# A decoder step: every second store of the finished y of groups 0 and 1 on ScalarE's queue, with new instruction orders

## The chip, the cores and the metric

The kernel runs on one core of one Trainium2 chip. The metric is device time in microseconds (us) of one execution. Before the change three runs gave 1998.69, 1999.23 and 3230.68 us; their median, 1999.23, is the time before. Engines are named as in the profile: PE is TensorE's matrix multiplication, PEld its weight load, DVE is VectorE, ACT is ScalarE, POOL is GpSimd, SP is SyncE, which here only issues DMAs.

## The reference, cut to what matters

One step of a decoder layer, in fp32, over 2048 prompt tokens and 8 sample tokens (2056 in all), with D_MODEL 1024 and D_FF 2816:

```python
def _rmsnorm(x, g):
    return x * lax.rsqrt(jnp.mean(x * x, axis=-1, keepdims=True) + EPS) * g

def _layer(x, ...):
    z = _rmsnorm(x, norm1_g) @ w_in          # split: RG-LRU branch, gelu gate, q, k, v
    rec = rglru(causal_conv(xr)) * gelu(gr)  # gated linear recurrence over the tokens
    att = sliding_window_attention(q, k, v)  # itself and 128 tokens back, learned sinks
    mix = concat(_rmsnorm(rec, rec_norm_g), _rmsnorm(att, attn_norm_g))
    h = x + mix @ w_out
    hn = _rmsnorm(h, norm2_g)
    y = h + (silu(hn @ w_gate) * (hn @ w_up)) @ w_down
    return y, ...

y_prompt = _rmsnorm(yp, final_norm_g)        # the same for y_sample
```

The change touches the last two lines, the feed-forward network (FFN) with its residual and the final norm. The caches and states that the step also returns are left out here.

## The kernel before

**Layout.** Activations are held transposed: 128 partitions are 128 features, the free dimension is tokens. An fp32 matrix product is done as three PE products of a high and a low part (hi x hi, hi x lo, lo x hi), so each weight tile is made as a pair: ACT casts the high part (L1903 in `keep_weights`, L1972 in `split_parts`), and POOL or DVE subtracts it to get the low part (L1904, L1973).

**Phases.** Up to some 600 us the kernel works on the input projection, the two head groups and the output projection; their result h goes to DRAM (`hs`). The rest is the FFN over three groups of tokens (`HALVES`): group 0 has 688 tokens, groups 1 and 2 have 684, each in two halves of 344 or 342 (n = 0, 1). Within a group, eleven pairs (`NPAIR`) of 128-wide chunks of D_FF are worked off:

- `mixed_weights` loads the weights of a pair; in group 0 it makes sums of their blocks and stores them to DRAM (`split_g`, `split_u`), from where groups 1 and 2 load them (L1927, 512 KB each).
- `products` multiplies gate ("g") and up ("u") by a Strassen-like scheme with seven block products instead of eight, in the order of `PRODS` = 1, 2, 6, 5, 7, 3, 4. Each is 12 matmuls into a PSUM bank. ACT copies the banks of products 1, 6 and 5 out (L2110, L2115, L2117), DVE adds the others.
- `down_parts` multiplies the result by w_down in the same way, in 14 rounds, each with two outputs of three matmuls. After each one DVE adds the PSUM bank into the tile y (L2175). Four of these chains share a set of PSUM banks, so a round can begin only when DVE has emptied the bank that it writes to. Pair 10 of each group and the first three pairs of group 0 use the plain `down` with 16 products (L2146).

**y.** The 16 pieces of y of a group (8 chunks of 128 features by 2 halves, 128 x 344 fp32 or 172 KB each) lie three to a tile in six tiles of the pool `bigp`. `y_load` (L1893 to L1899) loads them from h in DRAM, the residual; the down products are added to them; `finish` (L2177 to L2196) norms and stores them. `finish` runs once for each half of groups 0 and 1 and is called f01, f00, f11 and f10 (group, half; half 1 is done first, since the last `down` makes it first). For each half it squares and adds up the eight pieces, has PE sum over the partitions, and brings the row of norms over all partitions with `dram_bcast`: the row goes to DRAM and comes back broadcast as `rb_f` (L1152 to L1157). Then for each of the eight pieces DVE multiplies by gain and norm (L2195, a scalar_tensor_tensor), and SP stores the piece to the output (L2196). The tile is then used for the next group's y, whose load has to wait until the stores of the old pieces in it have landed. So at the passage from group 0 to 1 and from group 1 to 2, 16 multiplications, 16 stores and 16 loads meet the first products of the next group. Group 2 has a function of its own, `finish_last`, which already issues every second store of half 0 on ACT (L2243).

**The order of the work.** Each engine works off its instructions in order, and that order is written out by hand: `ORDER` (L106 to L852) is a dictionary with a list for each of PE, DVE, ACT, POOL and SP; `order` and `order_engines` (L1079 to L1095) turn the lists into dependencies. The tokens are these:

- On DVE, ACT, POOL and SP a token is the name of a chain, the generator that makes the instruction: `f11` is `finish` of group 1, half 1; `y2` is `y_load` of group 2; `wu2.1` is `mixed_weights` of up, group 2, pair 1; `wd2.0` the down weights, `pu2.1` `products` of up, `d2.0` `down_parts` of group 2, pair 0. Each token takes the next instruction that this chain has on this engine; `+k` takes the one that stands k further on among those left, and `:n` takes n in a row.
- On PE a token is a product: `u2_1_4:10` is ten matmuls of up, group 2, pair 1, product 4; `g2_2_1` is gate of pair 2; `w2_0_6_1:3` the three matmuls of the down round of product 6, column 1, group 2, pair 0; `st_` and `tr_` are the small ones of the norms.

The same lists also give the number of filler matmuls (`FILLS`, L854) that PE runs in the first 100 us while weights are being split.

A store that goes to another queue is thus in another engine's list: it must be named in ACT's list and vanish from SP's. An instruction that issues a DMA waits on its engine until the data is there, and all that stands behind it in that engine's list waits too.

Of the kernel before, what the change touches and what calls it, by code (L numbers as in the profile page):

```python
# [961 lines left out]
def hybrid_step(tc, xT, xR, vecs, cst, gatew, win, wout, wgate, wup, wdown, kT, vC, ck, cv, sconv, sh0,  # L962
                yT, pkT, pvT, pconv, phs, skw, svw, sconv_o, sh_o):
    nc = tc.nc
# [3 lines left out]
    with ExitStack() as ctx:  # L968
# [888 lines left out]
        with ExitStack() as bctx:  # L1857
# [319 lines left out]
            def finish(gi, n, t, dt):  # L2177
# [14 lines left out]
                for m in range(KD):  # L2192
                    yield t + dt * (F_FIN[2] + F_FIN[3])
                    v = ys[gi, n, m]
                    nc.vector.scalar_tensor_tensor(v, v, col(V_GF + m), bc[:, :nn], ALU.mult, ALU.mult)  # L2195
                    nc.sync.dma_start(yT[:, m, o:o + nn], v)  # L2196
# [187 lines left out]
```

## Time and profile before

| what | value |
|---|---|
| runs | 1998.69, 1999.23, 3230.68 us; median 1999.23 |
| profiled execution | 1999.11 us, of which the span of the profile is 1997.0 us |
| mean granted clock of PE | 0.997 of full speed |
| PE busy | 1971.0 us, 99% of the span, 12112 matmuls |
| DVE busy | 1560.6 us, 78% |
| ACT, POOL busy | 981.3 us, 49%; 959.8 us, 48% |
| DMA | 461.93 MB, 231 GB/s on average over the span |
| L2196, the stores | 32 instructions, issued by SP from 1137.5 to 1602.5 us |

The run of 3230.68 stands alone; the profiled execution agrees with the other two. PE is the engine to look at: where it idles, the end of the kernel moves, and where another engine idles, that tells nothing by itself. In rows by stretch, the first column is the stretch in us from the start of the span, then its length, then the busy time of PE, weight load, DVE, ACT and POOL with the count of instructions, then the granted clock, the share of the DMA engines and GB/s. In a timeline row the first figure is the start of a run of like instructions in us, the second their length, then engine, line, operation, output and inputs, form and count; the brackets give the idle time ahead of it and what ended it. "SPq" and "ACTq" are the parts of SP and ACT that issue DMAs. In rows of waits stand the waiting instruction, what released it, and then total us, count and longest.

### The profile page before, as it was taken

The numbers are of one execution on the slowest core, as the hardware profiler recorded it, in microseconds if no ns is written. First come the engines' busy times: TensorE is split into PE (matmuls) and PEld (weight loads), VectorE is DVE, ScalarE is ACT, GpSimd is POOL, SyncE is SP. The second block draws the span as 40 slices with busy tenths as digits, with TensorE's granted clock in tenths as the row PEclk, the third lists the DMA queues.
The fourth block names the chain that finished last, engine by engine and source line by source line (L and its number), as shares of the span: only waits on it lengthen the run. The fifth ranks groups of instructions, "written<-read, shape, count | busy, mean of one in ns | idle before, by whom it ended". The sixth has DMA issues, their size and how long they took to land. (4 is left out here: it accounts for less than half of the span.)

```text
span 1997.0 us, 34846 instructions
## 1 busy us (share of the span) xinstructions
PE 1971.0 (99%) x12112; PEld 1874.8 (94%) x12112; DVE 1560.6 (78%) x2894; ACT 981.3 (49%) x2032; POOL 959.8 (48%) x821
## 2 busy tenths in 40 slices
PE   8999999999999999999999999999999999999998
PEld 8988898888877999999999999999999999999998
DVE  7887986777986888888998786886668586766776
ACT  6775774664664534444446433433345433433433
POOL 5412362130233896788998754534456423322323
PEclk9999999999999999999999999999999999999999
DMA  8873586576688978655667886776558675565552
GB/s 314 287 252 138 194 300 198 183 254 210 223 283 291 335 263 268 220 215 210 246 241 279 265 289 231 234 237 210 191 191 267 228 259 199 179 211 195 180 181 103
DMA packets 218470, 461.93 MB, mean 231 GB/s; under 512 B 26230, under 2 KB 90406, under 8 KB 218278
## 3 DMA queue, kind: packets, MB, share of 16 engines
q1 hardware_dynamic: 214662, 456.69, 67.4%
q10 hardware_dynamic: 3632, 3.02, 0.4%
q8 instruction: 95, 1.56, 0.3%
q14 instruction: 81, 0.66, 0.1%
HBM read 345.51 MB, written 115.17 MB: 231 GB/s over the span
## 5 line engine op out<-in xcount | busy, mean ns | idle before, releaser
L1070 PE MATMUL ps_g<-hn,w_g 128*128 128x342 f32 (+1 forms) x2772 | 569.4, 320 | 0.3 <-DMA w_g<-split_g 0.3
L1070 PE MATMUL ps_u<-hn,w_u 128*128 128x342 f32 (+1 forms) x2772 | 559.5, 320 | 1.5 <-DMA w_u<-split_u 0.9
L1070 PEld LDWEIGHTS ps_g<-hn,w_g 128*128 128x128 f32 x2772 | 461.3, 188 | 1.2 <-ACT wd L1972 0.5
L1070 PEld LDWEIGHTS ps_u<-hn,w_u 128*128 128x128 f32 x2772 | 459.5, 188 | 3.0 <-ACT c_u L2115 1.6
L2175 DVE TENSOR_TENSOR y<-y,pw 128x342 f32<-128x342 f32 (+1 forms) x756 | 359.1, 504 | 114.7 <-PE pw L1070 108.4
L1070 PE MATMUL ip<-xn,w_in 128*128 128x512 f32 (+1 forms) x1680 | 365.2, 357 | 6.1 <-ACT xn L1105 5.7
L1070 PEld LDWEIGHTS ip<-xn,w_in 128*128 128x128 f32 x1680 | 269.6, 189 | 45.8 <-ACT xn L1105 5.7
L1070 PE MATMUL pw<-fh,wd 128*128 128x342 f32 (+1 forms) x864 | 253.4, 320 | 0.5 <-DVE y L2175 0.5
L1070 PE MATMUL pw<-t,wd 128*128 128x342 f32 (+1 forms) x972 | 243.7, 320 | 2.8 <-DVE y L2175 2.7
L1070 PE MATMUL op<-mix,w_out 128*128 128x512 f32 (+1 forms) x960 | 205.8, 355 | 0.4 <-ACT mix L1544 0.4
L1070 PEld LDWEIGHTS op<-mix,w_out 128*128 128x128 f32 x960 | 157.5, 189 | 25.3 <-ACT mix L1544 0.8
L1070 PEld LDWEIGHTS pw<-t,wd 128*128 128x128 f32 x972 | 169.9, 188 | 4.9 <-DVE y L2175 4.0
L1973 POOL TENSOR_TENSOR wd<-rd,wd 128x512 fp32r<-128x512 f32 x85 | 121.8, 1434 | 103.4 <-ACT wd L1972 99.1
L1972 ACT CAST wd<-rd 128x512 fp32r<-128x512 f32 x159 | 98.6, 621 | 130.0 <-PE ps_u L1070 39.8
L1070 PEld LDWEIGHTS pw<-fh,wd 128*128 128x128 f32 x864 | 158.6, 188 | 1.2 <-DVE y L2175 0.8
L1904 POOL TENSOR_TENSOR w_u<-ru,w_u 128x512 fp32r<-128x512 f32 x44 | 61.4, 1395 | 170.2 <-ACT w_u L1903 95.9
L1070 PE MATMUL pw<-fl,wd 128*128 128x342 f32 (+1 forms) x432 | 132.9, 320 | 0.0
L2089 DVE TENSOR_TENSOR c_u<-c_u,ps_u 128x342 f32<-128x342 f32 (+1 forms) x99 | 50.2, 508 | 101.2 <-PE ps_u L1070 93.9
L2071 POOL TENSOR_TENSOR c_u<-c_u,c_g 128x342 f32<-128x342 f32 (+1 forms) x60 | 65.4, 1090 | 124.8 <-DVE c_u L2089 115.1
L2060 DVE TENSOR_TENSOR fl<-c_u,fh 128x342 fp32r<-128x342 f32 (+1 forms) x132 | 105.4, 803 | 17.7 <-ACT fh L2059 17.0
L2059 ACT CAST fh<-c_u 128x342 fp32r<-128x342 f32 (+1 forms) x132 | 63.0, 480 | 110.6 <-POOL c_u L2071 49.3
L1070 PE MATMUL pd<-fh,w_d 128*128 128x344 f32 (+1 forms) x384 | 92.9, 320 | 0.0
(319 smaller groups left out, 3490.7 us busy)
## 6 DMA issues: line engine op xcount, KB each, us to landing
w_g<-split_g SPq DMA_DIRECT2D x88, 512.0 KB
w_u<-split_u SPq DMA_DIRECT2D x88, 512.0 KB
w_in<-split_w SPq DMA_DIRECT2D x84, 512.0 KB
rg<-in_wgate SPq DMA_DIRECT2D x110, 256.0 KB
ru<-in_wup SPq DMA_DIRECT2D x110, 256.0 KB
w_out<-split_w SPq DMA_DIRECT2D x48, 512.0 KB
split_g<-w_g SPq DMA_DIRECT2D x44, 512.0 KB
split_u<-w_u SPq DMA_DIRECT2D x44, 512.0 KB
```

The costliest lines, as they stand in the source:

```text
L1070: r = nc.tensor.matmul(*args, **kw)
L1904: lo_eng.tensor_tensor(w[:, 1, :], src, w[:, 0, :].bitcast(F32), op=ALU.subtract)
L1972: nc.scalar.copy(w[:, :, 0], v)
L1973: eng((E_DLO0, E_DLO1, E_DLO2)[gi][j]).tensor_tensor(w[:, :, 1], v, w[:, :, 0].bitcast(F32), op=ALU.subtract)
L2059: nc.scalar.copy(hi, v)
L2060: nc.vector.tensor_tensor(lo, v, hi.bitcast(F32), ALU.subtract)
L2071: (nc.vector if p == NPAIR - 1 or src is not v else eng(E_MUL[2 * h + n])).tensor_tensor(v, src, g, op=ALU.mult)
L2089: nc.vector.tensor_tensor(o, a, b, op)
L2175: nc.vector.tensor_tensor(v, v, ps, ALU.add)
```

## The change

One line of code changes, in `finish`: the pieces with odd m are stored by ACT's queue, the even ones still by SP's. That is 4 stores of each of f01, f00, f11 and f10, 16 in all. All five lists of `ORDER` are replaced: SP's has 1471 entries instead of 1487, ACT's 1903 instead of 1887, the others have the same instructions in another sequence. Most of the text of the lists differs only in where lines break; instructions really change places at the start (up to 50 us), around 550 to 650 us, in pairs 6 to 8 of group 0, and at the two passages between groups. The diff, cut to the code line and the lists at these passages:

```diff
@@ finish @@
                     nc.vector.scalar_tensor_tensor(v, v, col(V_GF + m), bc[:, :nn], ALU.mult, ALU.mult)
-                    nc.sync.dma_start(yT[:, m, o:o + nn], v)
+                    (nc.scalar if m % 2 else nc.sync).dma_start(yT[:, m, o:o + nn], v)
@@ ORDER, PE, group 1 to 2 @@
-u2_1_2:11 tr_f1_0 u2_1_2 u2_1_6:12 w2_0_2_0:3 u2_1_7:11 u2_1_5:12 u2_1_7 u2_1_3:12 u2_1_4:7 g2_2_1 u2_1_4 g2_2_1
-u2_1_4:4 w2_0_6_1:3 w2_0_6_0:3 g2_2_1:7 w2_0_1_3:2 g2_2_2 w2_0_1_3 g2_2_1:2 g2_2_2 g2_2_1 g2_2_2:9 w2_0_7_0:3 g2_2_2
-w2_0_7_1:3 w2_0_6_3:3 w2_0_3_0:3 w2_0_4_0:3 w2_0_3_1:3 w2_0_2_1:2 w2_0_4_1:3 w2_0_2_1 w2_0_5_2:3 w2_0_1_2:3 w2_0_7_3:3
+u2_1_2:11 tr_f1_0 u2_1_2 u2_1_6:12 w2_0_2_0:3 u2_1_7:11 u2_1_5:12 u2_1_7 u2_1_3:12 w2_0_6_1:3 w2_0_6_0:3 w2_0_1_3:3
+w2_0_7_0:3 w2_0_7_1:3 w2_0_6_3:3 w2_0_3_0:3 w2_0_4_0:3 w2_0_3_1:3 w2_0_2_1:2 w2_0_4_1:3 w2_0_2_1 w2_0_1_2:2 w2_0_7_3:2
+w2_0_1_2 w2_0_7_3 u2_1_4:2 w2_0_5_2:3 w2_0_2_2:3 u2_1_4:10 g2_2_1:2 g2_2_2 g2_2_1 g2_2_2 g2_2_1:2 g2_2_2:2 g2_2_1
...
@@ ORDER, DVE, group 0 to 1 @@
-f00+6 f00+5 f00+4 wu1.1 f00+3 f01 pu1.1 f00 d1.0 f00 wd1.0 d1.0+9 f00 pu1.0 d1.0+3 d1.0 wd1.0 f01 d1.0+2 d1.0+10
-d1.0:2 d1.0+2 d1.0 d1.0+9 d1.0+1 wd1.0 pu1.1+1 d1.0+1 d1.0+1 d1.0 d1.0+1 d1.0+8 pu1.1 d1.0+3 pu1.1+4 wg1.2 d1.0:2
+f01 f01+1 wu1.1 f00+5 f00+2 f00+5 f00+4 pu1.1 pu1.0 d1.0 f00+1 f00 wd1.0+1 f00 d1.0+9 d1.0 wd1.0+1 wd1.0 d1.0+2 f00
+pu1.1+1 d1.0+2 d1.0+10 f01 d1.0 d1.0+12 d1.0+3 d1.0 d1.0+2 d1.0 wd1.0 d1.0+1 d1.0:2 d1.0+1 d1.0+8 d1.0 d1.0+2 pu1.1
...
@@ ORDER, DVE, group 1 to 2 @@
-pg2.1 f10 pu2.0+1 wu2.1 wd2.0 pu2.0 pg2.1 pu2.0 pg2.1 wd2.0 f11+7 f11+2 f11+2 f11+3 pu2.1 f11+3 f11+2 f11:2 pu2.1+1
-f10+2 f10+4 f10+5 f10+4 f10 f10+2 d2.0+1 f10 d2.0 wg2.2 f10 d2.0+8 pu2.1+2 wg2.2 pu2.1+2 wd2.0 pu2.1+3 d2.0+2 d2.0+2
+pu2.0:2 pu2.0+1 f11 wu2.1 pu2.0+2 pu2.0:2 pg2.1 f10 pu2.0+1 wu2.1 wd2.0 pu2.0 pg2.1 pu2.0 pg2.1 wd2.0 f11+7 f11+3
+f11+3 f11+2 f11:2 f11+1 f11 pu2.1 f10+5 f10+2 f10+5 f10+4 f10+2 f10+1 d2.0 f10 d2.0 f10 pu2.1+1 pu2.1+2 pu2.1+2 d2.0+8
...
@@ ORDER, ACT, group 0 to 1 @@
-pg1.1 pu1.0 f00 wd1.0 wu1.1 pg1.1+2 pu1.1 wd1.0+1 wd1.0 pu1.0 wd1.0+1 pu1.1+1 wd1.0 pg1.1 pu1.1+1 wu1.1 pg1.1 wg1.2
+pg1.1 wd1.0+1 pg1.1 pu1.0+1 pu1.0 f00 wd1.0 wu1.1 f01+3 f01+2 pg1.1+2 pu1.1 wd1.0:2 f01 f00+2 pu1.0 f00+2 pu1.1+1
+pu1.1+1 f00 wd1.0 f00 f01 wd1.0 pg1.1 wu1.1 wg1.2 pu1.1 wg1.2 wd1.1 pu1.1 pg1.1 pg1.2 wd1.1:2 pu1.1:4 pg1.2+1 wd1.1
...
@@ ORDER, ACT, group 1 to 2 @@
-wu2.1 pu2.0 wd2.0 pu2.0+1 pu2.0 pg2.1+1 wu2.1 pg2.1:2 wd2.0 pu2.0 f11 pg2.1 wd2.0 pg2.1 wd2.0 pu2.1 pg2.1 f10 pu2.1+1
-wd2.0+1 pu2.1+1 wu2.1 wg2.2 wd2.0 wg2.2 pg2.2 wd2.1+1 pu2.1 wd2.1 pu2.1:2 wd2.1 pg2.2+1 pu2.1:2 wg2.2 pu2.1 wd2.1
+pg2.1:2 wd2.0 pu2.0 f11 pg2.1 wd2.0 pg2.1 wd2.0 pu2.1 f11+3 f10 f11 pu2.1+1 pg2.1 f11+1 pu2.1+1 f10+2 f10+2 f10+1 f10
+f11 wd2.0+1 wd2.0 wu2.1 wg2.2:2 wd2.1+1 pg2.2 pu2.1 wd2.1 pu2.1:2 wd2.1 pg2.2+1 pu2.1:2 wg2.2 pu2.1 wd2.1 pg2.2+1
...
@@ ORDER, SP, group 0 to 1 @@
-wd1.0+2 wd1.0+1 wd1.0+1 mix2 wg1.1 wu1.1 mix2 wg1.1 wd1.0+1 mix2:2 mix2+3 wg1.2 wu1.1+4 mix2+5 f01:2 wu1.1 f00 wd1.0+2
-mix2+3 wu1.1 f01+4 f00 f01+6 f01+1 wd1.1 f01+4 f01+1 wd1.0+1 wu1.1 f00+2 y1 f00+6 f00+5 f00+4 f01+2 y1:3 y1+1 y1+1
-y1+3 y1+4 y1+1 y1+1 f00+1 y1+1 f00 wd1.1+2 wg1.2 f01 y1 f00:2 f01 wu1.1 y1+1 wd1.1+1 wd1.1 y1 y1+1 y1 wg1.2 wg1.2+3
+mix2 wg1.1 wu1.1 mix2 wg1.1 wd1.0+2 mix2+5 mix2+1 mix2 wd1.0+1 wg1.2 wu1.1+4 mix2+5 f01 mix2+3 f01 wu1.1 f00 wd1.0+2
+wu1.1 wd1.1 f00 f01+3 f01+1 wd1.0+1 wu1.1 y1 f01+1 f00+1 y1+1 f00+2 y1:2 y1+2 y1+2 y1+3 y1+4 f01 wu1.1 y1+2 f00:2
...
@@ ORDER, SP, group 1 to 2 @@
-wd2.0:2 wg2.1:4 wd2.0 wg2.2 wd2.0:2 wu2.1+4 wd2.1 f11 wu2.1 f11 wg2.2 wd2.1 wu2.1+1 wu2.1 f11+7 f10 f11+2 wu2.1 f11+4
-f10 f11+2 f11+3 y2+2 f11+2 y2 f11+1 f11 y2 f10+2 f10+4 f10+5 f10+4 f10 f10+2 f10 y2 y2+2 y2+4 y2+5 y2+3 f10 y2+2 y2+2
+wu2.1+4 wd2.1 f11 wu2.1 f11 wg2.2 wd2.1 wu2.1+1 wu2.1 f10 wu2.1 f10 f11+2 y2+1 y2:2 f11+2 f11+1 f10+1 f10+2 y2 y2+2
+y2+4 y2+5 y2+2 f11 y2+2 f10+1 f10 y2+2 y2 wg2.2 y2+1 y2+3 y2+1 y2 wd2.1:3 wg2.2+1 wg2.2+2 y2 wd2.1 wg2.2 wd2.1 wu2.2
...
```

In words, at group 1 to 2: PE runs the twelve matmuls of up product 4 of pair 1 and the start of the next gate behind most of the down rounds of pair 0 (`w2_0_...`) instead of ahead of them; on ACT the eight stores stand among the casts and PSUM copies; on SP the stores that stood between the loads of up weights (`wu2.1`) are fewer. At group 0 to 1, PE's list moves four matmuls of up product 3 (pair 1) ahead of the last down rounds of pair 0; DVE's and SP's lists mix stores, loads of y and adds in another sequence.

More of the change, by code (lines that the diff above doesn't have):

```diff
@@ new lines @@
+pu0.9+3 pu0.9+1 d0.8 d0.9+1 pu0.9 pg0.10 d0.9 wd0.9 d0.9:2 wd0.9+1 pu0.9+1 pu0.9+1 wd0.9 pu0.9:2 d0.9 pg0.10 d0.9
+wu0.10 pg0.10 d0.9 d0.9+3 pu0.9 d0.9+1 d0.9:2 d0.9+4 d0.9+1 d0.9+1 d0.9+1 d0.9+2 wu0.10 d0.9+3 d0.9+2 d0.9+1 wd0.9
+wu0.10:2 d0.9 d0.9+2 d0.9+2 d0.9:2 pu0.10:2 hn1 wg1.0 d0.9 pu0.10 d0.9 d0.9+1 d0.9 hn1 pu0.10:2 pu0.10+1 hn1 pu0.10+1
+pu0.10:2 hl1 pu0.10:2 pg1.0 d0.10:3 hl1 d0.10:2 f01 d0.10:2 d0.10+1 d0.10 hl1 d0.10 hl1 d0.10 f01 f00 d0.10 d0.10+2
+wu1.0 f00 pg1.0 d0.10+1 d0.10 f01 d0.10 pg1.0 f01 f00 pu1.0 f00 mix2+1 mix2 wg1.1 mix2 pu1.0 mix2 pu1.0 pu1.0+1
@@ new lines @@
+pu0.9 wd0.9:2 wg0.10 pu0.9 wg0.10+1 pu0.9+2 wg0.10 wd0.9 pu0.9 pg0.10+1 pg0.10:2 pu0.9 wd0.9 wu0.10 pu0.9 wd0.9
+pg0.10:2 wu0.10 wu0.10+2 pg0.10 wd0.9 wu0.10:4 pu0.10 hn1:2 wg1.0 pu0.10 hn1+1 hn1 pu0.10 hn1+1 wg1.0 hn1+1 pu0.10
+wd0.10 hl1 wd0.10 hn1 hn1+1 hn1 wd0.10 hn1:2 pg1.0 pu0.10 hn1 pu0.10 hl1+2 hl1 wd0.10 pu0.10 hl1 hl1+2 hl1+1 hl1
+pg1.0+1 f01 hl1+1 hl1 f01+1 f01 wg1.0 hl1+2 pg1.0 hl1 f01 hl1:3 f00 hl1+1 wu1.0 hl1 f00 wu1.0 f00 f01:2 f00 pg1.0 f01
+f00 f01 f00 pg1.0:3 f00 wu1.0 f00 pu1.0 wg1.1:2 pu1.0+1 pu1.0:2 pg1.1 pu1.0 wg1.1 wd1.0 pu1.0 wu1.1 pu1.0 pg1.1+1 f01
@@ L771 @@
[L771 to L774 removed]
+pu0.9 wg0.10 wd0.9:3 wu0.10:3 wu0.10+1 wu0.10 wd0.9 wu0.10+1 wu0.10 hn1 wg1.0 hn1:2 hn1+1 hl1 wd0.10 hn1:5 wd0.10:3
@@ L775 @@
+hl1+3 hl1+1 hl1+1 hl1+1 f01 hl1 wg1.0 hl1+2 hl1+1 wu1.0 hl1 f01 f00 hl1 hl1+1 hl1 wd1.0 f01 f00 wd1.0+4 f00 wu1.0
+wg1.1 pu1.0:3 wd1.0 wg1.1 wu1.1 f01 pu1.0:2 f00 wd1.0:2 wd1.0+1 pu1.0 wd1.0+1 wd1.0+1 wd1.0 wd1.0+1 wd1.0 pu1.1 wu1.1
+pu1.1 wg1.2 wd1.1+5 wd1.1 wd1.1+1 wd1.1:2 pu1.1:3 wd1.1:2 pu1.1 wd1.1:2 wg1.2 wd1.1+1 wu1.2 wd1.1 wd1.2 wd1.2+4
+wd1.2+1 wd1.2+1 wu1.2 wg1.3 pu1.2 wd1.2 wd1.2+2 wd1.2+2 pu1.2 wd1.2 wd1.2+2 pu1.2 wd1.2 pu1.2:3 wg1.3 wd1.2 wu1.3:2
 wg1.4 pu1.3 wd1.3 pu1.3 wd1.3:2 pu1.3:4 wg1.4 wu1.4 wd1.3 wu1.4 wg1.5 pu1.4 wd1.4:2 pu1.4:4 wd1.4 pu1.4 wg1.5 wd1.4
@@ L852 @@
+wd2.7 wg2.9 wu2.8+4 wd2.8 wg2.9 wd2.8 wu2.8 wd2.8 wd2.8+1 wu2.8 wd2.8 wu2.8:2 wg2.9+4 wu2.9 wd2.8 wg2.9:2 wd2.8 wg2.9
+wu2.9 wg2.9 wd2.8 wg2.10 wu2.9+4 wg2.10 wd2.9:3 wu2.9 wd2.9:2 wu2.9:3 wg2.10+4 wu2.10 wd2.9+1 wg2.10:2 wd2.9 wg2.10
+wu2.10 wg2.10 wd2.9 wd2.10 wu2.10+4 wd2.10:2 wu2.10:3 wd2.10 wu2.10 f21:5 f21+1 f21+1 f21 f20:4
 """,
```

1350 lines of the change are left out of this document (666 added, 684 removed).

## The prediction

> **What bounds the kernel now.** I read the page's engine table first, then the busy time by stretches of the span, then the waits of TensorE (PE) in each stretch that has idle time, and last the timelines of the two places that the change touches.
>
> ```profile
> PE 1971.0 (99%) x12112; PEld 1874.8 (94%) x12112; DVE 1560.6 (78%) x2894; ACT 981.3 (49%) x2032; POOL 959.8 (48%) x821
> 10.00:100.00 90.00, 88.03 (x708) 85.61 (x707) 73.00 (x152) 65.30 (x141) 45.45 (x43) 1.00 0.88 305
> 1140.00:1160.00 20.00, 17.18 (x99) 15.14 (x98) 18.21 (x36) 5.30 (x11) 6.15 (x7) 1.00 0.94 302
> 1160.00:1580.00 420.00, 420.00 (x2679) 419.72 (x2678) 305.14 (x544) 174.06 (x361) 212.21 (x182) 1.00 0.68 227
> 1580.00:1615.00 35.00, 32.76 (x202) 31.03 (x201) 26.13 (x50) 8.94 (x19) 8.78 (x7) 1.00 0.91 292
> 1615.00:1950.00 335.00, 335.00 (x2134) 334.96 (x2134) 240.37 (x452) 130.26 (x258) 101.68 (x85) 1.00 0.59 195
> ```
>
> In the rows by stretch the first figures are the stretch and its length, then the busy time of PE, weight load, DVE, ACT and POOL, the granted clock, the DMA share and GB/s. PE is busy 1971.0 of 1997.0 us, so 26.0 us are all that any edit outside PE can win. The stores of groups 0 and 1 fall into 1140 to 1160 and 1580 to 1615, where PE idles 20.00 - 17.18 = 2.8 us and 35.00 - 32.76 = 2.2 us. Between and after them it idles 0.0 us. The change can therefore win at most 5.0 us there, 0.25%, while every us of new wait is paid in full, since PE has no slack to make it good. One matmul costs 335.00/2134 = 0.157 us.
>
> ```profile
> PE pw L1070 <- DVE y L2175: 1.9, 3, 0.7
> PE ps_u L1070 <- DMA w_u<-split_u: 0.9, 1, 0.9
> PE pw L1070 <- DVE y L2175: 1.4, 2, 1.2
> PE ps_u L1070 <- ACT c_u L2117: 0.4, 1, 0.4
> PE ps_g L1070 <- DMA w_g<-split_g: 0.3, 1, 0.3
> ```
>
> These are PE's waits, total, count, longest: two lines of the first stretch and three of the second. Most of it, 3.3 us, is PE waiting for DVE to add a down product into y (L2175) and so to free its PSUM bank. DVE is late because the 16 final multiplications (L2195) and the loads of the next y stand in its way.
>
> **What the change does to the queues.** 16 of the 32 stores of L2196 go from SP's queue to ACT's.
>
> ```profile
> L2196 SPq DMA_DIRECT2D out_yT<-y x32: 332/388/705, 1137.5 to 1602.5; - x32
> L2243 ACTq DMA_DIRECT2D out_yT<-y x4: 339/374/749, 1991.2 to 1992.8; - x4
> ```
>
> Shortest, median and longest issue in ns: SP sheds 16 x 0.388 = 6.2 us of issuing, ACT takes on 16 x 0.374 = 6.0 us, 3.0 us at each place. ACT is busy 5.30 of 20 us and 8.94 of 35 us there, so this lies beside PE and costs 0. What can cost is the order: ACT runs in order, and behind a store that waits for DVE's multiplication stand copies of PSUM that PE itself waits for (the 0.4 us above).
>
> The first place, SP's side:
>
> ```profile
> 1142.14 0.40 SPq L1927 DMA_DIRECT2D w_u<-split_u  x1
> 1144.52 2.21 SPq L2196 DMA_DIRECT2D out_yT<-y  x4
> 1147.09 6.03 SPq L1899 DMA_DIRECT2D y<-hs  x9
> SPq L1899 <- DMA w_u<-split_u: 0.9, 1, 0.9
> 1155.00:1160.00 5.00, 4.94 (x28) 4.41 (x29) 4.90 (x12) 1.01 (x2) 0.71 (x1) 1.00 1.02 330
> ```
>
> The nine y loads take 6.03 us to issue, 0.67 each instead of 0.39, and one of them waits 0.9 us for a weight load with which it shares no data: SP may have only so many transfers in flight, and the DMA engines are full (share 1.02 at 330 GB/s). A store is 172 KB, so 176/330 = 0.53 us of DMA time whichever queue issues it.
>
> [...]
>
> **The sum, first transition (group 0 to 1).** Before the w_u load at 1142.14 SP's old list has five stores of f01 behind the load of the product before it, the new list two. That brings the load forward by between 0 and 3 x 0.53 = 1.6 us, and its wait of 0.9 falls to between 0.9 and 0; I take 0.2. But this gain does not reach the end. Behind it PE waits three times for DVE's adds:
>
> ```profile
> 1149.47 0.50 DVE L2175 TENSOR_TENSOR y<-y,pw 128x342 f32<-128x342 f32 x1
> 1154.49 3.63 DVE L2175 TENSOR_TENSOR y<-y,pw 128x342 f32<-128x342 f32 x8
> 1155.05 1.21 PE L1070 MATMUL pw<-t,wd 128*128 128x342 f32 x6 [0.73 <-DVE y L2175]
> ```
>
> PE's third wait ends at 1155.05 with the add at 1154.49, which stands ten places behind the add at 1149.47. In the new DVE list the first add has two multiplications fewer ahead of it and one other operation more, 1.0 - 0.5 = 0.5 us earlier at best; but between the two adds stand eleven operations instead of nine, two at about 0.5 us. So the fifth add, and with it PE, comes out between 0.5 us early and 1.0 us late. I take 0.3 late. PE's list also moves four matmuls of up product 3 ahead of the last w rounds, which needs its weights some 4 us sooner; SP's list moves the load from behind 24 y loads and stores to behind 12 of them, 12 x 0.53 = 6.4 us sooner at best. I take 0 with a bound of +0.5. First transition: +0.3, from -0.9 (the w_u wait gone and nothing in its place) to +1.5.
>
> **Second transition (group 1 to 2).** Here the orders change more.
>
> ```profile
> 1593.65 3.26 PE L1070 MATMUL ps_u<-hn,w_u 128*128 128x342 f32 x19 [0.44 <-ACT c_u L2117]
> 1599.26 0.74 PE L1070 MATMUL pw<-t,wd 128*128 128x342 f32 x3 [1.24 <-DVE y L2175]
> 1600.16 0.73 PE L1070 MATMUL pw<-t,wd 128*128 128x342 f32 x3 [0.16 <-DVE y L2175]
> 1590.04 0.32 SPq L1156 DMA_DIRECT2D rb_f<-rows_f  x1
> 1583.15 2.03 DVE L2195 SCALAR_TENSOR_TENSOR y<-y,vec,rb_f 128x342 f32<-128x342 f32 x4 [0.77 <-DMA rb_f<-rows_f]
> 1594.07 4.71 DVE L2195 SCALAR_TENSOR_TENSOR y<-y,vec,rb_f 128x342 f32<-128x342 f32 x6
> 1598.70 0.50 DVE L2175 TENSOR_TENSOR y<-y,pw 128x342 f32<-128x342 f32 x1
> 1594.20 1.60 POOL L1904 TENSOR_TENSOR w_u<-ru,w_u 128x512 fp32r<-128x512 f32 x1 [3.12 <-DVE c_u L2089]
> ```
>
> Now PE runs up product 3 (12 matmuls from 1593.65), then product 4 and two matmuls of the next gate, 14 x 0.157 = 2.2 us, and only then w2_0_6_1, where it waits 1.24 us for the add at 1598.70. The new list puts all 14 behind the w rounds, because ACT's cast of product 4's weights now stands behind five stores. So PE arrives at w2_0_6_1 at 1593.65 + 12 x 0.157 = 1595.5.
>
> When is DVE there? Its six multiplications begin when the row broadcast has landed, 1594.07 now, 4.0 us after its issue. SP's list loses the three stores that stood between w_u loads ahead of that broadcast: 0 to 3 x 0.53 = 1.6 us sooner, I take 0.9, so 1593.2. Four multiplications take 2.03 us, 0.49 each; the six at 1594.07 took 4.71 while POOL ran beside them (1594.20). POOL's operation there subtracts the high part of a weight that ACT casts, and ACT's list has that cast later now, so I take 6 x 0.49 = 2.9, with 4.7 as the bound. Then come one add, a multiplication and the add that PE waits for: 0.42 + 0.49 + 0.50 = 1.4. That is 1593.2 + 2.9 + 1.4 = 1597.5, between 1596.8 and 1600.2: PE waits 2.0 us (1.3 to 4.7). After six matmuls (0.9 us) it needs the next bank, whose add stands behind a multiplication and three adds or products on DVE, 0.49 + 4 x 0.42 = 2.2 us: another 1.2 us (0.5 to 1.5). Against 1.24 + 0.16 + 0.28 = 1.7 now, the last being the wait for w_g, whose matmuls move back: +1.5, from +0.1 to +4.5.
>
> **The rest.** The new lists also permute single instructions in the first 100 us, around 550 to 650 and in pairs 6 to 8 of group 0. At the start SP loads the second half of a weight (256 KB, 0.8 us at 330 GB/s) ahead of an x tile, and some filler matmuls move. PE idles 2.0 us in 10 to 100. I take 0, bounded by one such transfer either way and rounded up: -1.0 to +1.0.
>
> **Sum.** The profiled execution took 1999.11 us, its span 1997.0 and 2.1 around it; the median of the runs is 1999.23, 0.1 above. 1999.1 + 0.3 + 1.5 + 0 = **2000.9 us**, no difference that a measurement of this kernel tells from none (about 2%, 40 us).
>
> **The rivals.**
>
> *The stalls go.* The y loads of the next group start sooner because half the stores no longer stand in front of them, and DVE's adds find their y and their turn. For it: 3.3 us of PE's waits are for these adds, and the new SP lists have y loads directly behind the second or third store. Against it: in 1155 to 1160 DVE is busy 4.90 of 5.00 us, so its adds wait for DVE's turn rather than for data. All waits gone would be 1999.1 - 2.8 - 1.7 = 1994.6; half of them gone, which I take, 1996.9.
>
> *Only issue time is saved.* The transfers are what is full, the stores' new queue changes nothing, and PE's and DVE's new orders cost and win alike. Then half of the 0.9 us wait for w_u goes: 1998.7. [...]
>
> *The clock drops: slower.* One long wait of PE costs more than itself:
>
> ```profile
> PE bc_at L1070 <- ACT rb_at L1140: 2.4, 1, 2.4
> 220.00:225.00 5.00, 5.00 (x18) 4.16 (x19) 3.74 (x7) 3.49 (x7) 1.75 (x3) 0.66 0.03 14
> ```
>
> After the single wait of 2.4 us before it, the stretch 220 to 225 was granted 0.66 of the clock: 0.34 x 5 = 1.7 us more. [...] The point from which it decides is a wait at w2_0_6_1 of 2.4 us or more, that is DVE's add after 1597.9, only 0.4 later than I take it. ACT can bring that about as well: if a store at its head holds up the PSUM copy ahead of product 3. With a wait of 3.5, midway between 2.4 and 4.7: 3.5 + 1.2 - 1.7 + 1.7 + 0.3 = +5.0, so 2004.1. For it: the bounds reach far above it; against it: the three waits of 0.5 to 0.7 us at 1150 to 1155 came in pieces and left the clock at 1.00.
>
> **How the numbers follow.** Forecast 0.40, with its own range 1999.2 to 2003; stalls go 0.18; issue time alone 0.20; clock drop 0.22. The range takes in the first two rivals' times and most of the third's bounds: 1996.6 to 2005.2, which leaves out under 0.2, the fuller win towards 1994.6 and waits near the upper bounds with the clock drop. All four lie within 2%. For over 2% either way 40 us would have to come from somewhere: a win of 40 exceeds all idle time, 26.0, so 0.005; a loss of 40 would need a hold-up that repeats in every pair, where the orders are nearly unchanged, so 0.015; within 2% 0.98.
>
> **What would show it.** Right: out_yT issues on ACT, 16 of them, about 0.4 us each; in the second transition one PE wait of about 2 us for DVE y directly behind up product 3 and a second near 1.2, with w_g's 0.3 gone; in the first the wait for w_u under 0.5 and the sum of PE idle near 3 us; 0.0 idle between and after. Wrong: PE idle under 1.5 us in both stretches together with y loads landing sooner (first rival), a clock row under 1.00 behind 1600 (third), PE waiting for an ACT copy for over 1 us, or idle time that appears where nothing of the stores is near.

## The result and the profile after

The changed kernel took 2003.39 us (median of 17 runs) against 1999.08 of before (17 runs beside them). The ratio is 1.0024, interval 1.0017 to 1.0031: 4.8 us slower, from 3.4 to 6.2. The single runs of 3230.68 us here and of 2749.80 in one of the experiments stand far from all others and are left out of the ratios. The result lies within 2% and inside the range given, but it is not the forecast of +1.8: it is near that of the third rival, the clock drop, at +5.0. The profiled execution took 2005.35 us, its span 2003.5.

The rows by stretch of the changed kernel, cut as for before (stretch, length, busy PE, weight load, DVE, ACT, POOL, clock, DMA share, GB/s), under the page's engine row:

```profile
PE 1974.9 (99%) x12112; PEld 1880.3 (94%) x12112; DVE 1556.0 (78%) x2894; ACT 980.2 (49%) x2032; POOL 956.1 (48%) x821
...
1140.00:1160.00 20.00, 16.85 (x92) 15.45 (x92) 17.84 (x33) 4.17 (x9) 6.71 (x6) 0.91 0.93 305
1160.00:1580.00 420.00, 420.00 (x2678) 419.63 (x2678) 303.58 (x547) 174.38 (x363) 211.91 (x182) 1.00 0.69 227
1580.00:1615.00 35.00, 29.95 (x170) 28.39 (x169) 22.48 (x44) 7.41 (x16) 7.42 (x6) 0.90 0.83 275
1615.00:1950.00 335.00, 335.00 (x2134) 334.96 (x2133) 239.82 (x452) 130.91 (x260) 101.66 (x85) 1.00 0.59 196
```

As before, PE idles nowhere between and after the two passages. Inside them two things are new. PE idle grows from 2.2 to 5.05 us in the second passage and by 0.3 in the first. And the granted clock, 1.00 in both places before, is 0.91 over the first 20 us and 0.90 over the second 35. PE's *busy* time grew by 3.9 us with the same 12112 matmuls: matmuls that run slower count as busy, so the busy share does not show this loss; the clock column does. In short stretches of the second passage:

```profile
1600.00:1602.50 2.50, 1.65 (x6) 1.21 (x6) 2.47 (x6) 1.78 (x4) 1.08 (x1) 0.72 0.76 237
1602.50:1605.00 2.50, 1.46 (x5) 1.46 (x6) 2.03 (x5) 0.41 (x1) 2.50 (x3) 0.50 0.93 267
```

In steps of 0.25 us the clock falls to 0.50 at 1601.1 and is back at 1.00 at 1607.9.

The stores moved as the diff says, 16 to each queue:

```profile
L2196 ACTq DMA_DIRECT2D out_yT<-y x16: 338/339/397, 1138.9 to 1600.3; - x16
L2196 SPq DMA_DIRECT2D out_yT<-y x16: 332/386/544, 1139.8 to 1604.2; - x16
```

PE's waits, first passage and then second:

```profile
PE ps_u L1070 <- ACT c_u L2115: 1.2, 1, 1.2
PE pw L1070 <- DVE wd L1973: 1.0, 1, 1.0
PE pw L1070 <- DVE y L2175: 0.9, 2, 0.7
...
PE pw L1070 <- DVE y L2175: 4.5, 2, 3.2
PE ps_u L1070 <- ACT c_u L2117: 0.4, 1, 0.4
```

The timeline of the second passage, by engines (start, length, work, count; in brackets the idle time ahead):

```profile
1595.26 2.14 PE L1070 MATMUL ps_u<-hn,w_u 128*128 128x342 f32 x12 [0.44 <-ACT c_u L2117]
1600.58 1.65 PE L1070 MATMUL pw<-t,wd 128*128 128x342 f32 x6 [3.18 <-DVE y L2175]
1603.55 0.65 PE L1070 MATMUL pw<-fh,wd 128*128 128x342 f32 x1 [1.31 <-DVE y L2175]
1604.56 2.77 PE L1070 MATMUL pw<-t,wd 128*128 128x342 f32 x9
1612.23 1.72 PE L1070 MATMUL ps_u<-hn,w_u 128*128 128x342 f32 x10
...
1596.19 3.00 DVE L2195 SCALAR_TENSOR_TENSOR y<-y,vec,rb_f 128x342 f32<-128x342 f32 x6 [7.26 <-DMA rb_f<-rows_f]
1600.02 0.50 DVE L2175 TENSOR_TENSOR y<-y,pw 128x342 f32<-128x342 f32 x1
...
1596.80 3.88 ACTq L2196 DMA_DIRECT2D out_yT<-y  x5
1601.77 0.61 ACT L1903 CAST w_u<-ru 128x512 fp32r<-128x512 f32 x1
...
1603.80 1.28 POOL L1904 TENSOR_TENSOR w_u<-ru,w_u 128x512 fp32r<-128x512 f32 x1
```

And two rows of the kernel before that were not shown:

```profile
1593.50 0.62 ACT L1903 CAST w_u<-ru 128x512 fp32r<-128x512 f32 x1
...
1601.96 0.32 PE L1070 MATMUL pw<-fh,wd 128*128 128x342 f32 x1
```

The passage begins 1.60 us later than before (ACT's first PSUM copy in it starts at 1585.00 instead of 1583.40). With that taken off, PE's two rounds behind DVE's adds start at 1598.98 and 1601.95. In the kernel before these were 1599.26 and 1601.96: **nearly the same two moments.** The first is set by DVE's add in both kernels. The second is set by DVE only now; before, PE came to it behind seven matmuls without a wait. In a second trace of the changed kernel, shown further down, the two rounds start 1.3 and 1.7 us earlier than before, counted from the start of the passage, and the passage is slow all the same. So it is not the rounds that come late. What differs is what PE does until then. Before, it ran 14 matmuls ahead of the first round and seven between the two; now it runs none: its new list has them behind the rounds, and up product 4's weights are cast behind five stores (1601.77 instead of 1593.50). The 21 matmuls, 21 x 0.157 = 3.3 us, come later and cover nothing. Then the nine matmuls at 1604.56 take 2.77 us, at a granted clock of 0.50; in "fill, both" below, at 1.00, the same nine take 1.59.

### The profile page after: what moved, and what is told of

The parts are those of the page before. It is cut to its first block, busy times and chain, and to the rows that moved or that the text cites. A ratio compares the mean times of both kernels' runs of the same rounds, so it can differ in the third digit from the quotient of the medians.

```text
span 2003.5 us, 34849 instructions
## 1 busy us (share of the span) xinstructions
PE 1974.9 (99%) x12112; PEld 1880.3 (94%) x12112; DVE 1556.0 (78%) x2894; ACT 980.2 (49%) x2032; POOL 956.1 (48%) x821
## 4 chain that ended last, share of the span: by engine, by line
PE 93%; DVE 4%; DMA 2%; ACT 1%; issue 1%; POOL 0%; SPq 0%; DVEq 0%; ACTq 0%; POOLq 0%
PE ps_g L1070 21%; PE ps_u L1070 21%; PE pw L1070 18%; PE ip L1070 14%; PE op L1070 7%; PE pd L1070 5%; PE s L1070 1%; PE o L1070 1%; PE pt L1075 1%; PE g L1070 1%; DMA split_g<-w_g 1%; DVE xc L1457 1%; DVE y L2195 0%; DMA n<-hs 0%; DMA mixed<-n 0%
## 5 line engine op out<-in xcount | busy, mean ns | idle before, releaser
L1973 POOL TENSOR_TENSOR wd<-rd,wd 128x512 fp32r<-128x512 f32 x85 | 121.2, 1426 | 110.9 <-ACT wd L1972 110.9
L1903 ACT CAST w_g<-rg 128x512 fp32r<-128x512 f32 x99 | 60.9, 621 | 67.4 <-PE pw L1070 24.0
```

What stands on the lines that cost most here:

```text
L1903: nc.scalar.copy(w[:, 0, :], src)
L1973: eng((E_DLO0, E_DLO1, E_DLO2)[gi][j]).tensor_tensor(w[:, :, 1], v, w[:, :, 0].bitcast(F32), op=ALU.subtract)
```

## The experiments

Theory A: the new orders of PE and DVE, most of all in the second passage, uncover waits for DVE, and the clock drops behind them. Theory B: ACT's queue costs. Rival C: the waits alone cost, the clock is a sign of them. Rival D: late transfers and casts cost.

Whole executions scatter by some 2 us, as much as what is looked for, so each trace is also read between marks. (A trace shows one execution, and in several kernels one of the shorter ones: 2001.19 us against a median of 2004.32 in "changed, again", 1999.45 against 2001.11 in "fill, both".) The first passage is counted from ACT's copy L2110 of gate pair 1 to that of up pair 2 in group 1, the second from up pair 1 to gate pair 3 in group 2. Line numbers of some experiments are one higher or lower. In before the marks are

```profile
L2110 ACT COPY c_g<-ps_g x1: 445/445/445, 1119.3 to 1119.3; 128x342 f32<-128x342 f32 x1
...
L2110 ACT COPY c_u<-ps_u x1: 447/447/447, 1193.9 to 1193.9; 128x342 f32<-128x342 f32 x1
...
L2110 ACT COPY c_u<-ps_u x1: 446/446/446, 1583.4 to 1583.4; 128x342 f32<-128x342 f32 x1
...
L2110 ACT COPY c_g<-ps_g x1: 445/445/445, 1649.9 to 1649.9; 128x342 f32<-128x342 f32 x1
```

so 74.6 and 66.5 us. For all kernels (ratio to before with interval; "new" where the passage has all or some of the changed orders):

| kernel | ratio | first passage | second passage |
|---|---|---|---|
| before | 1 | 74.6 | 66.5 |
| changed | 1.0024 [1.0017, 1.0031] | new 75.7 | new 71.4 |
| changed, again | 1.0018 [1.0009, 1.0026] | new 76.2 | new 70.4 |
| first passage only | 1.0005 [0.9996, 1.0014] | new 75.6 | 67.4 |
| second passage only | 1.0019 [1.0011, 1.0028] | 74.4 | new 70.9 |
| queue only | 1.0006 [0.9997, 1.0015] | 74.8 | 67.5 |
| orders only | 1.0038 [1.0024, 1.0052] | new 76.9 | new 72.6 |
| PE and DVE, second | 1.0032 [1.0021, 1.0044] | 74.2 | new 73.9 |
| fill, second | 1.0020 [1.0011, 1.0028] | new 76.2 | filled 69.9 |
| fill, both | 1.0012 [1.0002, 1.0022] | new 76.3 | filled 68.7 |
| first, stores late | 1.0022 [1.0012, 1.0032] | new 76.0 | 66.3 |
| first, load behind | 1.0007 [0.9998, 1.0016] | new 76.2 | 66.0 |
| PE and DVE, first | 1.0051 [1.0038, 1.0064] | new 85.2 | 67.1 |
| fill far away | 0.9997 [0.9988, 1.0006] | 74.8 | 66.8 |

**Which passage, queue or order.** Four kernels take the change apart: one passage or the other, the queue without the orders, the orders without the queue. In the passage kernels and in "queue only" the store's line is

```diff
-                    nc.sync.dma_start(yT[:, m, o:o + nn], v)
+                    (nc.scalar if m % 2 and gi in (0,) else nc.sync).dma_start(yT[:, m, o:o + nn], v)
```

with (0,), (1,) or (0, 1); "orders only" leaves that line as before and takes the changed lists.

> The kernel before with only the group 0 to 1 passage of the changed one: the stores of f01 and f00 with odd m on ACT's queue and all five orders of that passage. Everything else as before. In the profiled execution of the changed kernel this passage costs 1.25 us against before: 0.33 us more PE idle and a granted clock of 0.91 in 1140 to 1160. Theory A (the new orders cost, mostly in the group 1 to 2 passage): +1.2 us, ratio about 1.0006, clock below 1.00 somewhere in 1150 to 1160. Theory B (ACT's queue itself costs, the same at both passages): +2 us, half of the whole +4.3.

> The kernel before with only the group 1 to 2 passage of the changed one: the odd stores of f11 and f10 on ACT's queue and all five orders of that passage (and the few permutations behind it). Theory A: this passage carries the loss, +4.9 us or ratio 1.0025: one PE wait of about 3.2 us for DVE's add behind up product 3, a second of 1.3, and a clock near 0.5 for some 6 us after it. Theory B: +2 us, half of the whole.

> The orders of before on PE, DVE and POOL, and on SP and ACT too except that the 16 odd stores are taken out of SP's list and put into ACT's at the place where SP issued them in the profile of before. Theory A: nothing, -0.5 to +0.5 us, since PE's 14 matmuls stay ahead of the wait for DVE's add. Theory B: about +4 us as in the changed kernel, because ACT's copies and casts stand behind stores. If it is faster by 1 us or more, the queue does what the first rival of the prediction said (the y loads come sooner).

> All five orders of the changed kernel, but the 16 odd stores stay on SP's queue: they are taken out of ACT's list and put into SP's at the place where ACT issued them in the profile of the changed kernel. Theory A: as slow as the changed kernel, +4 us or ratio about 1.002, with the same long PE wait at the group 1 to 2 passage and the same clock drop. Theory B: 0.

Measured: +1.0 us (-0.8 to +2.8) for the first passage alone, +3.8 (2.2 to 5.6) for the second, +1.2 (-0.6 to +3.0) for the queue alone, with both passages at the upper end of what the old orders took elsewhere (74.2 to 74.8, 66.0 to 67.4), and +7.6 (4.8 to 10.4) for the orders alone. That is theory A. Theory B falls as the main cause: with the stores on SP the new orders do at least as badly. What the queue costs by itself cannot be told from nothing. The stretches of the two passages, first in "orders only" and then in "queue only":

```profile
1140.00:1160.00 20.00, 16.97 (x83) 15.28 (x83) 17.58 (x34) 3.04 (x6) 4.69 (x4) 0.83 0.93 293
1595.00:1610.00 15.00, 10.77 (x43) 10.14 (x44) 12.35 (x27) 1.57 (x3) 2.42 (x2) 0.66 0.78 250
```

```profile
1140.00:1160.00 20.00, 17.11 (x101) 15.44 (x100) 19.25 (x35) 4.64 (x10) 6.73 (x6) 1.00 0.96 323
1595.00:1610.00 15.00, 13.14 (x70) 12.39 (x70) 13.09 (x24) 3.74 (x7) 4.06 (x3) 0.89 0.93 308
```

The last column but two is the clock: under the new orders it falls in both places, under the old ones with the stores on ACT only a little, in the second (in before it stands at 1.00 in both).

**PE's and DVE's orders by themselves, second passage.** The lists of PE and DVE are the changed ones from the passage on, all else is before:

```diff
 PE
-u2_1_3:12 u2_1_4:7 g2_2_1 u2_1_4 g2_2_1 u2_1_4:4 w2_0_6_1:3 w2_0_6_0:3 g2_2_1:7 w2_0_1_3:2
+u2_1_3:12 w2_0_6_1:3 w2_0_6_0:3 w2_0_1_3:3
...
```

> The kernel before with only PE's and DVE's orders of the changed kernel at the group 1 to 2 passage; the stores stay on SP, and the orders of SP, ACT and POOL are those of before. (PE's order alone is not free: DVE's order of before has the product of up product 4 ahead of adds that PE's new order needs sooner.) Theory A: these two orders are the loss, since PE gives up the 21 matmuls that stood in the waits: a wait of 3 us or more behind up product 3, a clock drop, +4 to +5 us. Rival D (the late broadcast of the row, 0.5 us later behind the store traffic of two queues, and the late casts are the loss): at most +1.

Measured: +6.4 us (4.2 to 8.8), the passage 73.9, its waits and its stretch:

```profile
PE pw L1071 <- DVE y L2176: 4.9, 3, 3.2
PE ps_u L1071 <- DMA w_u<-split_u: 1.1, 1, 1.1
...
1595.00:1610.00 15.00, 10.19 (x43) 8.86 (x44) 12.07 (x26) 1.76 (x3) 0.91 (x1) 0.77 0.90 285
```

The long wait and the clock drop are there with no store moved and ACT's casts early: theory A, and the late casts of rival D fall as the main cause. The late broadcast does not fall by this run, since DVE's six multiplications began 11.7 us behind the first mark of the passage here and 10.7 in before. It falls by the second trace of the changed kernel (next): there they began 10.2 behind it, and the passage still took 70.4. The time is more than expected; 1.1 us of it is a wait for w_u that the kernel before does not have in this passage.

**Has the clock a price of its own?** Only filler matmuls are added to the changed lists; their products are overwritten. In "fill, second":

```diff
-u2_1_3:12 w2_0_6_1:3 w2_0_6_0:3 w2_0_1_3:3
+u2_1_3:12 w_ps_g2_2_1:20 w2_0_6_1:3 w2_0_6_0:3 w_ps_g2_2_1:9 w2_0_1_3:3
```

and in "fill, both" also

```diff
-u1_1_7:3 w1_0_1_3:3
+u1_1_7:3 w_ps_g1_2_1:5 w1_0_1_3:2 w_ps_g1_2_1:8 w1_0_1_3
```

> The changed kernel with 29 filler matmuls (256 wide, ones by ones, into the free PSUM bank that the first product of the next gate will overwrite) at the group 1 to 2 passage: 20 ahead of w2_0_6_1, where PE waits 3.18 us, 9 ahead of w2_0_1_3, where it waits 1.31. Work is only added; at 0.157 us for 342 columns one filler is about 0.12, so 2.4 and 1.1 us, both inside the waits. If the clock drop behind the waits costs time of its own (theory A: 2.2 of the 4.9 us), the clock stays at 1.00 in 1600 to 1610 and the kernel is 2 us faster than the changed one: about +2 over before, ratio 1.001. If only the waits cost (rival C), it is as slow as the changed kernel or up to 1 us slower: ratio 1.0024 or above.

> As the run with 29 fillers, with 13 more at the group 0 to 1 passage: 5 ahead of w1_0_1_3 (a wait of 0.68 us) and 8 ahead of its third matmul (1.04 us). Theory A: the clock stays at 1.00 in 1150 to 1160 too, another 1 to 1.5 us faster: +0.5 to +1 over before. Rival C: no faster than the changed kernel, +4 to +5.

> The changed kernel unaltered, for a second trace of it. Theory A: the group 1 to 2 passage again takes 4 to 5 us more than in the trace of before (4.93 in the first trace), with a wait of about 3 us and a clock drop; the group 0 to 1 passage 1 to 2 us more (1.06), the clock drop there not in every execution since its waits are short. If the loss of the second passage were chance of one execution, it would come out under 2.

In the second trace of the changed kernel the second passage took 3.9 us more than in before, just under the 4 to 5 expected, with waits of 2.15 and 0.91. That trace, then those of "fill, second" and "fill, both" (stretch first, then PE's timeline):

```profile
1595.00:1610.00 15.00, 12.57 (x59) 11.55 (x60) 12.33 (x25) 3.42 (x6) 4.93 (x4) 0.77 0.80 265
...
1596.52 1.39 PE L1070 MATMUL pw<-t,wd 128*128 128x342 f32 x6 [2.15 <-DVE y L2175]
1598.82 0.65 PE L1070 MATMUL pw<-fh,wd 128*128 128x342 f32 x1 [0.91 <-DVE y L2175]
1608.14 1.72 PE L1070 MATMUL ps_u<-hn,w_u 128*128 128x342 f32 x10
```

```profile
1595.00:1610.00 15.00, 13.73 (x89) 12.45 (x88) 13.04 (x29) 3.42 (x6) 4.37 (x4) 1.00 0.87 283
...
1598.82 1.22 PE L1070 MATMUL pw<-t,wd 128*128 128x342 f32 x6
1604.85 0.42 PE L1070 MATMUL pw<-fh,wd 128*128 128x342 f32 x1 [0.79 <-DVE y L2175]
1609.83 1.72 PE L1070 MATMUL ps_u<-hn,w_u 128*128 128x342 f32 x10
```

```profile
1595.00:1610.00 15.00, 14.55 (x95) 13.69 (x94) 14.19 (x28) 3.43 (x6) 5.23 (x4) 1.00 0.94 306
...
1594.38 2.55 PE L1071 MATMUL ps_g<-ones 128*128 128x256 f32 x20
1596.77 1.12 PE L1071 MATMUL pw<-t,wd 128*128 128x342 f32 x6
1597.73 1.24 PE L1071 MATMUL ps_g<-ones 128*128 128x256 f32 x9
1606.54 1.72 PE L1071 MATMUL ps_u<-hn,w_u 128*128 128x342 f32 x10
```

From the first round behind the wait to up product 4 the changed kernel needs 1612.23 - 1600.58 = 11.65 us in its first trace and 1608.14 - 1596.52 = 11.62 in its second; with nine matmuls more inside it, the filled ones need 1609.83 - 1598.82 = 11.01 and 1606.54 - 1596.77 = 9.77, at a clock of 1.00. In the longer one PE ran into DVE's next adds and waited for them (0.47 and 0.79 us). So **the clock drop has a price of its own, 0.6 to 1.9 us here**, and work without any use wins it back. Rival C falls by these traces, two on each side. By the times it stays unproven: +4.0 (2.2 to 5.6) and +2.4 (0.4 to 4.4), where +2 and +0.5 to +1 were expected, overlap with the changed kernel's +4.8 and +3.6 (1.8 to 5.2). The 13 fillers of the first passage did not help: PE waited 1.9 us for ACT's copy ahead of them, and the clock stood at 0.91 again.

The first passage of "fill, second" is that of the changed kernel, with no filler in it:

```profile
1140.00:1160.00 20.00, 15.35 (x89) 13.49 (x88) 19.21 (x35) 4.93 (x10) 7.16 (x6) 1.00 0.96 316
```

The clock kept 1.00 there, PE idled 4.65 us, and the passage took 76.2 all the same. So in the first passage the clock drop is not shown to cost anything.

**Why is the first passage slower?** Two edits of the "first passage only" kernel, on ACT and on SP (in brackets the store that a token stands for):

```diff
 ACT (stores f01 m 1, f00 m 5 and 7 behind the PSUM copy pu1.1)
-pu1.1 wd1.0:2 [f01 m1] [f00 m5] pu1.0 [f00 m7] pu1.1+1 pu1.1+1
+pu1.1 wd1.0:2 pu1.0 pu1.1+1 [f01 m1] [f00 m5] [f00 m7] pu1.1+1
 SP (load wd1.1 behind the broadcast f00)
-wu1.1 wd1.1 f00
+wu1.1 f00 wd1.1
```

> The kernel with only the new group 0 to 1 passage, but on ACT three stores (f01 m 1, f00 m 5 and 7) are moved behind the PSUM copy L2115, which PE's up product 7 waits for and which stood behind them. If the stores at ACT's head are what holds up PE there (1.8 us of wait in that kernel's profile), this wait falls under 1.0, where the load of w_u may take its place (0.9 in the profile of before), the clock stays at 1.00 in 1140 to 1155, and the kernel is 1 to 2 us faster than with the stores ahead: 0 to -0.5 against before. If DVE's adds set the passage's end anyway, the wait moves to pw and the time stays at +1.2.

> The kernel with only the new group 0 to 1 passage, but on SP one load of the next down weights (wd1.1, L1984), which the new order has ahead of the row broadcast of f00 and the old one behind it, is put behind it again. In the traces with the new passage DVE's first multiplication of f00 comes 9.9 to 11.1 us after ACT's copy of the row, in those with the old one 8.3 to 8.9. If that load ahead of the broadcast is what delays it, the first multiplication comes within 9.3 us, the passage takes under 0.5 us more than before and the clock stays at 1.00 in 1140 to 1160. If it is the new order of DVE's work and of the y loads, the passage still takes 1 us or more with a clock drop.

The wait for ACT's copy did go (first row "first passage only", then two of "stores late"), and moved:

```profile
PE ps_u L1071 <- ACT c_u L2116: 1.8, 1, 1.8
```

```profile
PE pw L1071 <- DVE y L2176: 2.6, 3, 1.2
PE pw L1071 <- DVE wd L1974: 1.1, 1, 1.1
```

The passage stays at 76.0 and the clock drops. So the held-up copy is real and does not set the end; what PE waited for instead was DVE. (The ratio of 1.0022 is more than this trace explains, 1.4 us in the first passage and none in the second; the traced execution, 1998.91, is the shortest of its runs, whose median is 2003.80. The rest stays open.) With the load behind the broadcast DVE's first multiplication of f00 came 11.35 us after the copy of the row, not under 9.3, and the passage took 76.2: that guess fell too.

One wait is common to the new orders: PE waits 0.5 to 1.8 us for the low part of a down weight (L1973) in seven of the eight traces with all of them, and in none of the five with the old ones. In DVE's old list this subtraction stands right behind the first add into y and one multiplication, in the new one six places further back (before, then changed; the passage of the changed kernel starts 0.55 us later):

```profile
1150.63 0.68 DVE L1973 TENSOR_TENSOR wd<-rd,wd 128x512 fp32r<-128x512 f32 x1
```

```profile
1153.09 0.68 DVE L1973 TENSOR_TENSOR wd<-rd,wd 128x512 fp32r<-128x512 f32 x1
```

No run moved it back, so whether it sets the end of the passage is not shown.

> The kernel before with only PE's and DVE's orders of the changed kernel at the group 0 to 1 passage; stores on SP, the orders of SP, ACT and POOL those of before. From the first PSUM copy of gate pair 1 to that of up pair 2 the kernels with all of the passage's new orders took 1.0 to 2.3 us more than before, those with the old orders -0.4 to +0.2. Theory A (orders of PE and DVE): +1 to +2 here too. Rival (ACT's copy behind stores is the loss of this passage): within 0.4 of before, since ACT holds no store.

This kernel has, for the first passage, what "PE and DVE, second" has for the second: only PE's and DVE's new lists. Its +10.2 us and 85.2 did not tell its theories apart, for a cause that neither had:

```profile
PE ps_u L1071 <- DMA w_u<-split_u: 9.2, 2, 5.9
```

PE's new list needs up product 3's weights sooner, and SP's old list loads them late. The lists of a passage belong together: PE's and DVE's alone cost 10.2 us here.

**A wait far from all stores.**

```diff
-bc_at0_0:4 ip1_7_0:7 pt5_0_0 ip1_7_0 bc_at0_4
+bc_at0_0:4 ip1_7_0:7 pt5_0_0 ip1_7_0 w_op0_0_0:18 bc_at0_4
```

> The kernel before with 18 filler matmuls (256 wide, into the bank that the first output projection will overwrite) inside the wait of 2.35 us for the second row broadcast of the attention norm near 217 us, far from every store. 18 x 0.12 = 2.1 us fit into the wait. If a wait's clock drop has a price of its own (theory A), the rows of 220 to 225 stand at 1.00 instead of 0.79 and 0.53, and the stretch behind is 1.7 us sooner in executions that drop the clock: ratio 0.9992 or so, below 2 us of scatter between executions and so read from the trace. If not, nothing or +0.3.

The stretch 215 to 225 in before, in "first passage only" (the same code there) and with the fillers:

```profile
215.00:225.00 10.00, 7.65 (x33) 6.14 (x32) 8.25 (x12) 4.51 (x9) 3.50 (x6) 0.83 0.46 157
```

```profile
215.00:225.00 10.00, 7.70 (x45) 6.47 (x44) 9.00 (x12) 4.91 (x10) 3.49 (x5) 1.00 0.44 157
```

```profile
215.00:225.00 10.00, 9.68 (x62) 8.43 (x61) 8.83 (x12) 4.94 (x10) 3.32 (x5) 1.00 0.45 157
```

The fillers keep the clock at 1.00. But the same wait of 2.3 us without fillers left it there too in three of twelve traces, and this trace's first mark, 1121.2, is the latest of all. The time, -0.6 us (-2.4 to +1.2), shows nothing either way. No version was shown to beat the kernel before.

## Why the prediction was right and wrong

*The place and the bound* held: no time over 2% could move, PE idles only at the passages, and the queue by itself costs nothing measurable (6 us of issuing beside PE, as costed). But the loss did not show as idle time alone: part of it is busy time at a granted clock of 0.50 (1601.1 to 1607.9 in the changed kernel).

*Second passage, +1.5 from +0.1 to +4.5.* The mechanism was right: 14 matmuls leave the gap and PE meets DVE's add bare. The six multiplications took 3.00 us (2.9 taken), the second wait was 1.31 us in the first trace of the changed kernel and 0.91 in the second (1.2 taken), and the wait for w_g was gone. Two terms were off. The multiplications were taken to begin 0.9 us sooner, with the broadcast. Counted from the start of the passage they began 0.5 later in the first trace and 0.5 sooner in the second, so PE waited 3.18 and 2.15 us instead of 2.0. (The row of before, 1594.07, does not show when its broadcast landed: it has no idle time ahead. DVE had last been waiting for ACT's copy, up to 1593.63.) And the clock was left out of the forecast: "the point from which it decides is a wait at w2_0_6_1 of 2.4 us or more". In the second trace 2.15 us sufficed: the clock fell to 0.50 at 1597.4, ahead of the second wait, which began at 1597.9. The passage costs 71.3 - 66.8 = 4.5 us (mean of the four unfilled traces with all of the new orders against the seven with the old ones); by the fillers 0.6 to 1.9 of it is the clock. The third rival had 4.7 for this passage, with waits of 3.5 and 1.2 and a single drop of 1.7; in the traces the waits were shorter and the drop twice as long (0.23 x 15 = 3.5). So its mechanism was there, and that its total fits so well is in part luck. It had a chance of 0.22, although the forecast's own wait lay only 0.4 under its point of decision.

*First passage, +0.3 from -0.9 to +1.5.* Measured 76.1 - 74.6 = 1.6 (eight traces with all of its new orders, though two have a list edited and one fillers, against five), just past the bound. PE's idle time in 1140 to 1160 is 3.3 us on average instead of 2.8, but the clock there was under 1.00 in seven of the eight and at 1.00 in all five. The argument against the third rival, that waits in pieces had left the clock alone, did not hold: in three of the seven only pieces of 0.6 to 1.2 us came ahead of the drop. In the other four it was a single wait of 1.8 to 2.0. But the loss of this passage is not thereby the clock's, as "fill, second" shows with its 76.2 us at 1.00. The term that was mis-sized is the 0.3 for the new orders, 1.6 measured; one wait that it does not have is PE's for the down weight (0.5 to 1.8 us). The prediction's sign of error "PE waiting for an ACT copy for over 1 us" came (1.2), but in the run with the stores behind the copy the passage stayed as long without it. The wait for w_u, taken as 0.2, was absent in one trace of the changed kernel and 1.9 us in the other. That SP may have only so many transfers in flight was a guess from one wait of 0.9 us in before; no run tests it. Which entries of DVE's or SP's list delay this passage stays open.

*The rest, 0 from -1 to +1.* The first mark stands at 1117.4 us on average in the five traces with the new start and at 1118.3 in the eight with the old one and no filler: -0.9, where single traces have a standard deviation of 1.6, so it is not clear of the scatter. Sum by traces: 1.6 + 4.5 - 0.9 = +5.2, against +4.8 by the times.

*The first two rivals.* Neither came. The stalls did not go: PE's idle time in the two places grew by 0.3 and 2.8 us. The second rival was right that the queue changes little (+1.2, -0.6 to +3.0, in "queue only") and wrong that the new orders cost and win alike (+7.6 in "orders only").

## What to carry to other kernels

Matmuls that stand ahead of a wait are its cover: here 21 of them, 3.3 us by 0.157 us each, were moved behind two rounds that start at nearly the same moments as before or earlier, and the passage took 4.5 us longer on average, 0.6 to 1.9 of it by the clock. On a PE-bound kernel read the granted clock in steps of a few us wherever PE waits 1 to 3 us (it fell to 0.50 behind a single wait of 1.80 us in "first passage only" and behind 2.15 and 3.18 us in the changed kernel), and put a price on the clock as soon as the estimated wait comes near the length that once dropped it; one trace of one wait is no threshold: the same wait of 2.3 us dropped it in nine of twelve traces and left it at 1.00 in three. An instruction order written by hand is one object: judge a list with the lists that feed it.

## What the runs showed of the hardware

In these traces the clock is lost in portions. Read in steps of 0.25 us, the column of the granted clock stands at 1.00 or at 0.50, and between them only in the step in which it changes. A drop lasts 3.4 us or two or three times that: from 221.5 to 224.9 in before, from 1154.0 to 1157.4 and from 1601.1 to 1607.9 in the changed kernel and, by the means of 0.69, 0.50 and 0.79 over the three stretches of 5 us from 1595 on, from 1596.9 to 1607.1 in "orders only". A portion of 3.4 us at 0.50 is 1.7 us of PE's work, and so the stretches have it: 0.17 x 10 = 1.7 us at 215 to 225, 0.09 x 20 = 1.8 at 1140 to 1160, 0.11 x 15 = 1.7 at 1595 to 1610 in "queue only", and twice and three times that at 0.77 (3.5) and 0.66 (5.1). How much of it the kernel's time shows is another matter: 0.6 to 1.9 us of the 3.5 in the second passage; at full clock PE met DVE's adds sooner and waited for them (0.47 and 0.79 us in "fill, second").

The same wait does not always cost a portion: the wait of 2.3 us for the broadcast at 217 us did in nine of twelve traces of unchanged code. In the second passage a wait of 2.15 us did, in the first a wait of 1.80 in "first passage only" and three of 0.7 to 1.2 in the changed kernel; waits of 1.25, 0.83 and 1.75 in "fill, second" did not. What decides between them no run shows.
